# A hybrid encoder layer: memory, x and the S5 parameters laid out by features and by state on the host, packing through three buffers

## The chip, the cores and the metric

The kernel runs on one core of a Trainium2 chip. The metric is device time in microseconds (us) of one execution; a lower figure is better. Times are compared as medians of several runs. The profile is one execution, recorded by the hardware profiler, with the engines TensorE (PE, and PEld for its weight loads), VectorE (DVE), ScalarE (ACT), GpSimd (POOL) and SyncE (SP). SP and POOL also issue DMA transfers, each on a queue of its own.

## The reference

One layer is applied to two groups of tokens, 256 of a prompt and 512 of a sample, together 768 tokens of 1024 features (`TILES = 6` tiles of 128 tokens), each group with a memory of 256 rows of its own (together 512). All is in fp32.

```python
def layer(x, mem, ...):
    h = rmsnorm(x, norm_mix_g)
    u, q, k, v, qm, gl = jnp.split(h @ w_in, SPLITS, axis=-1)
    s5_out   = ...  # bidirectional S5: 64 groups of 16 channels, 64 complex states, + s5_d * u, half-GLU
    diff_out = ...  # differential attention over the tokens, 8 heads
    mem_out  = memory_attention(qm, rmsnorm(mem, mem_norm_g), w_mem_kv, mem_q_g, mem_k_g)
    ...             # branches times w_branch, gates from gl, sum, times w_out, residual, SwiGLU FFN

def memory_attention(q, mem_n, w_kv, q_g, k_g):   # 4 heads of 256
    k, v = jnp.split(mem_n @ w_kv, 2, axis=-1)
    q, k = rmsnorm(q, q_g), rmsnorm(k, k_g)
    p = softmax((q @ k.T) * 256 ** -0.5)
    return p @ v
```

For each of the two directions S5 has `lam`, `dt`, `b` and `c`, with `lam_bar = exp(lam * dt)`, `b_bar = (lam_bar - 1) / lam * b`, and the states `s[t] = lam_bar * s[t-1] + b_bar * u[t]`, `y = real(c * s)`.

## The kernel before, in words

**Products.** Every fp32 operand is split into a high and a low fp32r part, and a product is three matmuls, high x high, high x low, low x high (`mm3`, lines 863 to 865). The splits are made by `split_evac` (853 to 859: high part on ACT, low part on DVE, with a factor per partition where one is given) and, for weights, by `WStream` (547). That class loads weights in halves of 128x1024 on SP's queue through three raw buffers (599), writes the high part on ACT (698) and the low part on DVE (704), in four buffers each, one weight ahead of the one in use (`get`, `ahead`).

**Order.** The program is written for a tile framework that gives every engine a fixed order of instructions, drawn up with a simulated timeline when the program is built; tiles come from pools with a number of buffers each, and an instruction that takes a buffer waits for its last reader. `keep_in_program_order` pins a few instructions to their place. Work of different kinds is interleaved by generators, and a `Pace` (rate times the units done) says when a generator makes a step: `PAR_RATE` for the S5 parameters, `MEM_RATE` for the memory attention, `PACK_RATE` for packing, `S5_RATE` for the S5 steps.

**The stages up to the change's end.**

- *Memory rows* (1087 to 1126). Four row tiles of memory are loaded on SP (`load_rows`, `nx`, six buffers), transposed on PE (1110, `nT`, four 128x128 blocks to a bank), and written with the gain `gmem` as `memThi`/`memTlo`. DVE squares the rows (1124) for the scale `mrs` of each memory row, which is applied later, when K and V leave PSUM.
- *Memory products.* `MEM_ORDER` (796) names twelve units: k0, k1, v0, v1, q0, k2, q1, v2, k3, q2, v3, q3. `mem_k` (957, PSUM `mk`) gives K of a head for four row tiles, `mem_v` (970, `mv`) first scales and normalizes K (with `mrs`) and then gives V (`Vh`, `Vl`), `mem_q` (989, `mq`) gives Q for all 768 tokens from H and transposes K (`kT`). The products of `k0` begin with the first half of the rows, with three filling matmuls (`warm`) ahead of them.
- *x and H* (1132 to 1162). Six row tiles of x are loaded on SP, ACT squares and sums them (885), DVE forms the reciprocal root in twelve small steps (836 to 850) and the normalized rows times gain (`norm_rows`, 906), PE transposes each (`to_features`, 894, `nT`, 48 transposes) beside k1, v0 and v1, and ACT and DVE write `Hhi` and `Hlo` (855, 856).
- *S5 parameters* (`S5.params`, 76). `lam` is loaded on SP, transposed on PE (127, `lamT`), and DVE, ACT and POOL form powers (`pwr`, `pwi`) and factors (`zr`, `zi`, `fr`, `fi`), beside the units k2 to q3 and the memory attention (1021; `ms` scores, `mp`, `mpT` transposes at 1076, `pTh`/`pTl`, `mo` output, stored to DRAM as `mo_scrh`, `mo_scrl`).
- *Raw B and C* (`S5.raws`, 59) are loaded near the end of these units, C on POOL (66), B on SP (73); B's source has 16 contiguous floats (64 bytes) to a piece.
- *Packing* (`S5.pack`, 262), four quarters beside the first two of four chunks of `u` (`u_chunk`, 1189; PSUM `u`). For each: four transposes of C on PE (295, `cT`), their copies on ACT (296), four copies of powers on ACT (301, 302), the diagonal of D and two complex products on DVE (269, pieces through `csc`), all into one buffer `par`, whose store to DRAM (`par_scr`, 312) is issued on SP. A later `fetch` (315) brings back 1/16 of all this at a time (`qd` 0 to 15).
- *S5 steps* (497) beside the rest of `u` and twelve chunks of `gl`: `_outer` (338) forms G (349, `ptG`) and E, then responses (`psK`) and so on.

Behind these follow the differential attention, the branches and the FFN, which the diff doesn't touch.

Of the kernel before, what the change touches and what calls it, by code (L numbers as in the profile page):

```python
# [24 lines left out]
class S5:  # L25
# [15 lines left out]
    def open_dram(self, ctx):  # L41
        tc = self.tc
        self.dr = ctx.enter_context(tc.tile_pool(name="s5d", bufs=1, space=DRAM))
        self.u_scr = [self.dr.tile([128, 8 * NK], F32, name=f"u_scr{m}") for m in range(8)]
        self.k_scr = [self.dr.tile([128, 240], F32, name=f"k_scr{m}") for m in range(16)]
        self.p_scr = [self.dr.tile([128, 4, NPAR], F32, name=f"par_scr{m}") for m in range(4)]
# [4 lines left out]
    @staticmethod  # L51
    def par_views(t):

        f = lambda a, b, **k: t[:, :, a:b].rearrange("p q (g x) -> p q g x", g=4)
        C, B = (t[:, :, o : o + 128].rearrange("p q (g c h) -> p q c g h", g=4, c=2) for o in (0, 128))
        Ar, Ai, Fr, Fi = (f(o, o + 32) for o in range(256, 384, 32))
        return C, B, Ar, Ai, Fr, Fi, t[:, :, 384:400]

    def raws(self, scratch):

        nc, A = self.nc, self.A
        self.craw, self.braw = [], []
        for nm in ("s5_c_re", "s5_c_im"):
            raw = scratch.tile([128, 8, 2, 64], F32, name=nm + "_raw")
            for d in range(2):
                nc.gpsimd.dma_start(raw[:, :, d, :], A[nm][0, d].rearrange("g h p -> (g h) p")
                                    .rearrange("(m q) p -> q m p", q=128))
            self.craw.append(raw)
        for nm in ("s5_b_re", "s5_b_im"):
            raw = scratch.tile([128, 64, 16], F32, name=nm + "_raw")  # L70
            self.braw.append(raw)
            for d in range(2):
                nc.sync.dma_start(raw[64 * d : 64 * d + 64], A[nm][0, d].rearrange("g p h -> p g h"))
                yield

    def params(self, scratch, psA):
# [29 lines left out]
        nc.sync.dma_start(self.kpos, self.consts["kpos"])  # L106
        lraw = []
        for nm in ("s5_lam_re", "s5_lam_im"):
            raw = scratch.tile([64, 2, 64], F32, name=nm + "_raw")
            nc.sync.dma_start(raw, A[nm][0].rearrange("d g p -> g d p"))  # L110
            lraw.append(raw)
        ldt = t("ldt")
        for d in range(2):
            nc.sync.dma_start(ldt[64 * d : 64 * d + 64, :],
                              A["s5_log_dt"][0, d].unsqueeze(0).to_broadcast([64, 64]))
        dcol = scratch.tile([128, 16], F32, name="s5dcol")
        nc.gpsimd.memset(dcol, 0.0)
# [4 lines left out]
        yield  # L122

        lam = []
        for nm, raw in zip(("lre", "lim"), lraw):
            ps = psA("lamT")
            nc.tensor.transpose(ps[:, 0:64], raw.rearrange("g d p -> g (d p)"), env.ident[0:64, 0:64])
            o = t(nm)
            nc.scalar.activation(o, ps[:, 0:64], AF.Copy)
            lam.append(o)  # L130
        lre, lim = lam
# [125 lines left out]
        dv = A["s5_d"][0].rearrange("(q g h) -> g h q", g=4, h=16)  # L257
        for g in range(4):
            nc.sync.dma_start(dcol[32 * g : 32 * g + 16], dv[g])
        self.lam = zr, zi, fr, fi, pwr, pwi, dcol  # L260

    def pack(self, scratch, psA):

        nc, env = self.nc, self.env
# [6 lines left out]
        zr, zi, fr, fi, pwr, pwi, dcol = self.lam  # L271
        split = lambda a: a.rearrange("p (q g) -> p q g", g=4)

        for qt in range(4):
            gs = slice(16 * qt, 16 * qt + 16)
            st = scratch.tile([128, 4, NPAR], F32, name=f"par{qt}", tag="par")
            C, B, Ar, Ai, Fr, Fi, dg = self.par_views(st)
# [13 lines left out]
            ps = psA("cT")  # L291
            for part, (raw, sgn) in enumerate(zip(self.craw, (1.0, -1.0))):
                for m in range(2):
                    o = 256 * part + 128 * m
                    nc.tensor.transpose(ps[:, o : o + 128], raw[:, 2 * qt + m].rearrange("q d p -> q (d p)"), env.ident)
                nc.scalar.activation(C[:, :, part], ps[:, 256 * part : 256 * part + 256]
                                     .rearrange("p (q g h) -> p q g h", g=4, h=16), AF.Copy, scale=sgn)
            yield
# [4 lines left out]
            for g in range(4):  # L303
                r = slice(32 * g, 32 * g + 32)
                tt(dg[r], dcol[r, 4 * qt : 4 * qt + 4].unsqueeze(2).to_broadcast([32, 4, 16]),
                   env.ident[r, 32 * g : 32 * g + 16].unsqueeze(1).to_broadcast([32, 4, 16]), mul)
            yield
            ir, ii = (x[:, gs].rearrange("p (q g) h -> p q g h", g=4) for x in self.braw)
# [421 lines left out]
def hybrid_block(ctx, tc, A, outs, consts):  # L730
# [357 lines left out]
    with tc.tile_pool(name="nrm", bufs=1) as pool, tc.tile_pool(name="nrmg", bufs=1) as pg:  # L1088
# [14 lines left out]
        for t0 in (0, 2):  # L1103
# [12 lines left out]
            if t0 == 0:  # L1116
# [3 lines left out]
                for _ in range(2):  # L1120
                    next(units)
# [1022 lines left out]
```

## Time and profile before

| what | value |
|---|---|
| median of 3 runs (lowest to highest) | 1756.37 us (1753.03 to 1759.49) |
| the profiled execution's own time | 1753.71 us |
| its span in the profile | 1751.9 us |
| mean granted clock of PE | 0.994 |
| DMA packets, bytes, mean rate | 217088, 247.44 MB, 141 GB/s |
| PE busy from 0 to 75 us, of 75.00 | 71.11 us |
| PE busy from 75 to 282.47 us, of 207.47 | 188.16 us |
| PE busy from 282.47 to the end, of 1469.43 | 1459.11 us |

The last three rows are an answer of the trace for three stretches: 75 us is about where Q of the memory attention begins, and at 282.47 us begins the first product behind the last transpose of C. The profile names each group of instructions by line, engine, operation and its tiles as out<-in. A bracket at a row's end holds the time that the engine stood idle before it and what ended this. In rows of the timeline, start and duration come first; matmuls are pipelined, so their durations overlap and their spacing is what counts. A DMA row gives the size of one transfer and the median time from issue to landing. SPq and POOLq are the queues of the issuing engines.

### The profile page before, as it was taken

The numbers are of one execution on the slowest core, as the hardware profiler recorded it, in microseconds if no ns is written. First come the engines' busy times: TensorE is split into PE (matmuls) and PEld (weight loads), VectorE is DVE, ScalarE is ACT, GpSimd is POOL, SyncE is SP. The second block draws the span as 40 slices with busy tenths as digits, with TensorE's granted clock in tenths as the row PEclk, the third lists the DMA queues.
The fourth block names the chain that finished last, engine by engine and source line by source line (L and its number), as shares of the span: only waits on it lengthen the run. The fifth ranks groups of instructions, "written<-read, shape, count | busy, mean of one in ns | idle before, by whom it ended". The sixth has DMA issues, their size and how long they took to land.

```text
span 1751.9 us, 30000 instructions
## 1 busy us (share of the span) xinstructions
PE 1718.4 (98%) x11405; PEld 1588.3 (91%) x11405; DVE 1337.7 (76%) x2486; ACT 941.2 (54%) x1933; POOL 289.1 (16%) x301
## 2 busy tenths in 40 slices
PE   9999897999999999999999999999999999999999
PEld 8989885889888999999998899998889898989897
DVE  6886666899999547898977596894678868787876
ACT  6464442865665436878766464552434544444441
POOL 0000000000000011100111120350023234343430
PEclk9999998999999999999999999999999999999999
DMA  8223655767756636566693445664304547475733
GB/s 256 86 67 109 109 150 156 160 171 186 176 148 174 154 84 150 125 142 146 166 214 106 139 147 165 160 176 146 85 25 120 150 107 180 123 166 133 174 112 108
DMA packets 217088, 247.44 MB, mean 141 GB/s; under 512 B 51304, under 2 KB 171376, under 8 KB 216944
## 3 DMA queue, kind: packets, MB, share of 16 engines
q1 hardware_dynamic: 174208, 155.59, 29.8%
q0 software_dynamic: 31792, 64.76, 19.8%
q10 hardware_dynamic: 10944, 25.17, 4.2%
q8 instruction: 90, 1.47, 0.4%
q14 instruction: 54, 0.44, 0.1%
HBM read 169.84 MB, written 53.35 MB: 127 GB/s over the span
## 4 chain that ended last, share of the span: by engine, by line
PE 81%; issue 11%; DMA 4%; DVE 2%; ACT 2%; POOL 0%; SPq 0%; POOLq 0%; ACTq 0%; DVEq 0%
PE br L864 4%; PE br L865 4%; PE br L863 4%; PE gate L864 3%; PE gate L863 3%; PE gate L865 3%; PE up L863 3%; PE up L864 3%; PE up L865 3%; PE dn L865 3%; PE dn L863 3%; PE dn L864 3%; PE qk L865 3%; PE qk L864 3%; PE qk L863 3%
## 5 line engine op out<-in xcount | busy, mean ns | idle before, releaser
L698 ACT ACTIVATE wh<-wr 128x1024 fp32r<-128x1024 f32 x118 | 133.8, 1138 | 69.5 <-PE gl L864 18.8
L863 PE MATMUL gl<-Hhi,wh 128*128 128x256 f32 (+1 forms) x384 | 132.8, 346 | 0.0
L704 DVE TENSOR_TENSOR wl<-wr,wh 128x1024 fp32r<-128x1024 f32 x72 | 96.1, 1338 | 47.4 <-ACT wh L698 47.0
L865 PE MATMUL gl<-Hhi,wl 128*128 128x256 f32 (+1 forms) x384 | 129.2, 337 | 0.0
L864 PE MATMUL gl<-Hlo,wh 128*128 128x256 f32 (+1 forms) x384 | 128.8, 336 | 0.0
L702 POOL DMA_DIRECT2D wl<-wr x46 | 39.4, 865 | 463.0 <-ACT wl L701 430.9
L863 PE MATMUL qk<-wh,Hhi 128*128 128x256 f32 x384 | 107.6, 280 | 0.0
L864 PE MATMUL qk<-wl,Hhi 128*128 128x256 f32 x384 | 107.6, 280 | 0.0
L865 PE MATMUL qk<-wh,Hlo 128*128 128x256 f32 x384 | 107.2, 279 | 0.0
L618 ACT ACTIVATE wh_S<-ws 128x512 fp32r<-128x512 f32 x91 | 53.9, 625 | 68.1 <-PE up L864 26.6
L623 DVE TENSOR_TENSOR wl_S<-ws,wh_S 128x512 fp32r<-128x512 f32 x91 | 68.0, 768 | 29.0 <-ACT wh_S L618 26.1
L863 PEld LDWEIGHTS gl<-Hhi,wh 128*128 128x128 f32 x384 | 72.1, 188 | 9.5 <-issue 2.2
L865 PEld LDWEIGHTS gl<-Hhi,wl 128*128 128x128 f32 x384 | 72.1, 188 | 8.5 <-issue 0.6
L864 PEld LDWEIGHTS gl<-Hlo,wh 128*128 128x128 f32 x384 | 72.2, 188 | 6.9
L863 PEld LDWEIGHTS qk<-wh,Hhi 128*128 128x128 f32 x384 | 72.3, 188 | 0.8
L865 PEld LDWEIGHTS qk<-wh,Hlo 128*128 128x128 f32 x384 | 72.3, 188 | 0.5
L864 PEld LDWEIGHTS qk<-wl,Hhi 128*128 128x128 f32 x384 | 72.2, 188 | 0.5
L1406 DVE TENSOR_REDUCE nm<-sc 128x1 f32<-128x512 f32 (+1 forms) x96 | 56.6, 597 | 15.1 <-PE sc L1401 14.2
L1408 ACT ACTIVATE p<-sc,nm 128x512 f32<-128x512 f32 (+1 forms) x96 | 59.0, 617 | 12.0 <-DVE nm L1406 11.5
L644 POOL TENSOR_TENSOR ws<-wr,ws 128x512 f32<-128x512 f32 x26 | 39.6, 1524 | 128.2 <-DVE wl_S L623 128.2
L618 ACT ACTIVATE wh_A<-wr 128x512 fp32r<-128x512 f32 x65 | 38.0, 622 | 37.6 <-PE up L864 15.7
L1585 DVE TENSOR_TENSOR fs<-fs,up 128x384 f32<-128x384 f32 x70 | 37.5, 548 | 24.7 <-PE up L865 23.9
(713 smaller groups left out, 6252.3 us busy)
## 6 DMA issues: line engine op xcount, KB each, us to landing
wr<-in_w_in_dram SPq DMA_DIRECT2D x48, 512.0 KB, 4.6
wl<-wr POOLq DMA_DIRECT2D x46, 512.0 KB, 5.5
wr<-in_w_gate_up_dram SPq DMA_DIRECT2D x44, 512.0 KB, 4.0
wr<-in_w_branch_dram SPq DMA_DIRECT2D x24, 512.0 KB, 4.0
wr<-in_w_down_dram SPq DMA_DIRECT2D x22, 512.0 KB, 4.4
wr<-in_w_mem_kv_dram SPq DMA_DIRECT2D x16, 512.0 KB, 3.7
wr<-in_w_in_dram SPq DMA_DIRECT2D x32, 256.0 KB, 4.2
p_scr<-de ACTq DMA_DIRECT2D x27, 256.0 KB, 4.4
```

The source lines that it names most:

```text
L618: self.nc.scalar.activation(f(hi), src, AF.Copy)
L623: self.nc.vector.tensor_tensor(out=f(lo), in0=src, in1=f(hi).bitcast(F32), op=ALU.subtract)
L644: gt(out=s4, in0=A12, in1=s2, op=sub)
L698: self.nc.scalar.activation(hi, r, AF.Copy)
L702: self.nc.gpsimd.dma_start(lo, r.bitcast(F32R), accum_op=ALU.add)
L704: self.sub.tensor_tensor(out=lo, in0=r, in1=hi.bitcast(F32), op=ALU.subtract)
L863: pe.matmul(ps, wh, xh, start=start, stop=False)
L864: pe.matmul(ps, wh, xl, start=False, stop=False)
L865: pe.matmul(ps, wl, xh, start=False, stop=stop)
L1406: v.tensor_reduce(out=nm[:, m : m + 1], in_=ps, axis=AX.X, op=ALU.max, negate=True)
L1408: act.activation(pm[:, 0:n], ps, AF.Exp, bias=nm[:, m : m + 1], accum_out=s1s[:, tt : tt + 1] if m == 0 else s2)
L1585: v.tensor_tensor(out=o, in0=x, in1=y, op=add)
```

## The change

- A new function `layouts` on the host makes `memT` and `xT` (features by tokens), the two gains as columns (`gcols`), `s5_lamT` (real, imaginary, log dt, by state), `s5_bT` (B by state, four quarters), and `s5_cd` (C by state and D's diagonal, 16 pieces).
- Memory features come from `memT` in four tiles on SP. K of head 0 is computed with the features as the outer loop, in four PSUM banks at once, as the features come. The rows of memory are loaded as well, on POOL's queue through two buffers (`load_row`, tag `row`), for the squares alone. The three filling matmuls go.
- x's rows are also loaded on POOL's queue through these two buffers, for the squares alone (ACT). x by features comes in four tiles on POOL's queue in the buffers of `memT`. Each token's reciprocal root is spread over all partitions by PE (ones times a diagonal, 128x128, `rsb`), then DVE multiplies x, gain and `rsb` for each of eight feature blocks of 128x768, and ACT and DVE split that into H.
- `params` loads `s5_lamT` in one transfer on POOL. `pack` loads B by quarters on POOL (two buffers), has no PE work, no C and no diagonal, uses three buffers `par`, stores on POOL, and begins earlier: at the unit where it loaded B and C before (the last units of `MEM_ORDER`), behind the rest of the parameters, at a rate of 0.8 in place of 1.45.
- `fetch` has two transfers on SP: C and diagonal from the input, the rest from what was packed. G's imaginary part is formed with its sign by a `scalar_tensor_tensor` in place of a `tensor_tensor`.

The diff, cut to its core:

```diff
 def params(self, scratch):
-        for nm in ("s5_lam_re", "s5_lam_im"):
-            raw = scratch.tile([64, 2, 64], F32, name=nm + "_raw")
-            nc.sync.dma_start(raw, A[nm][0].rearrange("d g p -> g d p"))
...
-            nc.tensor.transpose(ps[:, 0:64], raw.rearrange("g d p -> g (d p)"), env.ident[0:64, 0:64])
+        lam = scratch.tile([128, 3, 64], F32, name="s5lamT")
+        nc.gpsimd.dma_start(lam, A["s5_lamT"])
...
 def pack(self, scratch):
+        def load(qt):
+            raw = scratch.tile([128, 2, 16, 16], F32, name=f"s5b{qt}", tag="s5b", bufs=2)
+            nc.gpsimd.dma_start(raw, A["s5_bT"][qt])
+            raws.append(raw)
+        load(0)
+        load(1)
+        yield
         for qt in range(4):
-            st = scratch.tile([128, 4, NPAR], F32, name=f"par{qt}", tag="par")
+            st = scratch.tile([128, 4, NPAR - 144], F32, name=f"par{qt}", tag="par", bufs=3)
...
-                    nc.tensor.transpose(ps[:, o : o + 128], raw[:, 2 * qt + m].rearrange("q d p -> q (d p)"), env.ident)
-                nc.scalar.activation(C[:, :, part], ps[:, 256 * part : 256 * part + 256]
-                                     .rearrange("p (q g h) -> p q g h", g=4, h=16), AF.Copy, scale=sgn)
-            yield
             for dst, src in ((Ar, pwr), (Ai, pwi)):
                 lay = lambda x: x[:, :, gs].rearrange("p m (q g) -> p q g m", g=4)
                 nc.scalar.activation(dst[0:64], lay(src[0:64]), AF.Copy)
                 nc.scalar.activation(dst[64:128], lay(src[64:128, ::-1]), AF.Copy)
-            for g in range(4):
-                r = slice(32 * g, 32 * g + 32)
-                tt(dg[r], dcol[r, 4 * qt : 4 * qt + 4].unsqueeze(2).to_broadcast([32, 4, 16]), ...)
-            yield
-            ir, ii = (x[:, gs].rearrange("p (q g) h -> p q g h", g=4) for x in self.braw)
-            cscale(B[:, :, 0], B[:, :, 1], zr, zi, ir, ii, 16)
             yield
             cscale(Fr, Fi, fr, fi, Ar, Ai, 8)
-            nc.sync.dma_start(self.p_scr[qt], st)
+            yield
+            raw = raws[qt].rearrange("p c (q g) h -> p c q g h", g=4)
+            cscale(B[:, :, 0], B[:, :, 1], zr, zi, raw[:, 0], raw[:, 1], 16)
+            nc.gpsimd.dma_start(self.p_scr[qt], st)
+            if qt < 2:
+                load(qt + 2)
             yield
 def fetch(self, qd):
-        self.nc.sync.dma_start(t[:, 0], self.p_scr[hv][:, q])
+        self.nc.sync.dma_start(t[:, 0, 0:144], self.A["s5_cd"][qd])
+        self.nc.sync.dma_start(t[:, 0, 144:], self.p_scr[hv][:, q])
...
-PACK_RATE = 1.45
+PACK_RATE = 0.8
+    def load_row(pool, src, eng):
+        x = pool.tile([128, 1024], F32, name=uid("row"), tag="row", bufs=2)
+        eng.dma_start(x, src)
+        return x
...
+        W._dma()
+        for j in range(4):
+            if j == 2:
+                W._dma()
+            t = pool.tile([128, 2 * TOK], F32, name=f"mt{j}", tag="ft", bufs=4)
...
+            nc.sync.dma_start(t, A["memT"][:, 2 * j : 2 * j + 2])
...
+        pss = [psd("mk"), env.psa("mk"), psd("mk"), env.psa("mk")]
+        for k in range(8):
+            if k % 4 == 0:
+                W.ahead(0, 1 + k // 4)
+            split_evac(MT[0][:, k], MT[1][:, k], mt[k // 2][:, k % 2], cg[:, 0, k : k + 1])
+            w = [x[:, 256 * (k % 4) : 256 * (k % 4) + 256] for x in W.parts[0][k // 4]]
+            for tt in range(4):
+                t = slice(128 * tt, 128 * tt + 128)
+                mm3(pss[tt][:, 0:256], MT[0][:, k, t], MT[1][:, k, t], *w, k == 0, k == 7)
...
         for t in range(4):
-            tc.keep_in_program_order(v.scalar_tensor_tensor(out=xm[t], in0=xm[t], scalar=1.0, in1=xm[t], op0=mul,
+            xm = load_row(pool, ms[t], nc.gpsimd)
+            tc.keep_in_program_order(v.scalar_tensor_tensor(out=xm, in0=xm, scalar=1.0, in1=xm, op0=mul,
                                                             op1=mul, accum_out=mss[:, t : t + 1]))
...
         for tt in range(TILES):
-            to_features(norm_rows(pool, xr[tt], rs[tt], g), H, tt)
-            next(units)
+            xr = load_row(pool, xs[tt], nc.gpsimd)
+            tc.keep_in_program_order(square_sum(xr, pool, ss[:, tt : tt + 1]))
+            if tt % 3 == 2:
+                next(units)
+        for j in range(4):
+            t = pool.tile([128, 2 * TOK], F32, name=f"xt{j}", tag="ft", bufs=4).rearrange("p (k t) -> p k t", k=2)
+            nc.gpsimd.dma_start(t, A["xT"][:, 2 * j : 2 * j + 2])
+            xt.append(t)
+        mean_eps(ss, TILES, 1024)
+        rs = rsqrt(ss, TILES, "xrs")
+        for c0, n in ((0, 512), (512, 256)):
+            ps = env.psa("rsb")
+            for t in range(n // 128):
+                dg = pg.tile([128, 128], F32, name=uid("rsd"), tag="rsd", bufs=2)
+                tt = c0 // 128 + t
+                v.tensor_scalar(out=dg, in0=env.ident, scalar1=rs[:, tt : tt + 1], scalar2=None, op0=mul)
+                pe.matmul(ps[:, 128 * t : 128 * t + 128], ones2, dg, start=True, stop=True)
+            act.activation(rsb[:, c0 : c0 + n], ps[:, 0:n], AF.Copy)
+        for k in range(8):
+            x = xt[k // 2][:, k % 2]
+            v.scalar_tensor_tensor(out=x, in0=x, scalar=cg[:, 1, k : k + 1], in1=rsb, op0=mul, op1=mul)
+            split_evac(H[0][:, k], H[1][:, k], x)
+            next(units, None)
...
             if W.next == 12 and mctx is not None:
                 mctx.close()
                 mctx = None
+                par.drain()
                 scr = uctx.enter_context(tc.tile_pool(name="s5scr", bufs=1))
-                raws = s5.raws(scr)
-            if raws is not None:
-                next(raws, None)
-
-    par.drain()
-    for _ in raws:
-        pass
+                par = Pace(s5.pack(scr), PACK_RATE)
+                next(par.gen)
```

More of the change, by code (lines that the diff above doesn't have):

```diff
@@ L45, in open_dram @@
         self.k_scr = [self.dr.tile([128, 240], F32, name=f"k_scr{m}") for m in range(16)]
-        self.p_scr = [self.dr.tile([128, 4, NPAR], F32, name=f"par_scr{m}") for m in range(4)]
+        self.p_scr = [self.dr.tile([128, 4, NPAR - 144], F32, name=f"par_scr{m}") for m in range(4)]
     def open_work(self, ctx):
@@ L1134, in hybrid_block @@
+        nc.gpsimd.dma_start(gq, A["mem_q_g"][0].unsqueeze(0).to_broadcast([128, 256]))
+        for _ in mem_k(0, pss):
+            pass
         mean_eps(mss, 4, 1024)
@@ L2128 @@
     arrays, A, C = {}, {}, {}
-    for name in _INS:
-        a = np.ascontiguousarray(inputs[name])
+    given = {n: np.asarray(inputs[n]) for n in _INS}
+    laid = layouts(given)
+    for name in [n for n in _INS if n not in _LAID] + list(laid):
+        a = np.ascontiguousarray(laid[name] if name in laid else given[name])
         arrays[f"in_{name}_dram"] = a
```

184 lines of the change are left out of this document (69 added, 115 removed).

## The prediction

> **What bounds the kernel now.** I read the page, then what PE waits for in the first 310 us, then busy time by stretch, then PE, DVE, ACT and the DMA issues in order of time.
>
> ```profile
> span 1751.9 us, 30000 instructions
> PE 1718.4 (98%) x11405; PEld 1588.3 (91%) x11405; DVE 1337.7 (76%) x2486; ACT 941.2 (54%) x1933; POOL 289.1 (16%) x301
> ```
> ```profile
> PE cT L295 <- ACT par L296: 11.7, 1, 11.7
> PE mpT L1076 <- DVE mss L1065: 4.8, 1, 4.8
> ...
> PE u L863 <- ACT par L296: 1.3, 1, 1.3
> ...
> PE mpT L1076 <- DVE mol L856: 0.7, 1, 0.7
> ```
> ```profile
> 200.00:225.00 25.00, 20.80 (x110) 18.20 (x111) 16.56 (x37) 11.54 (x19) 0.28 (x6) 0.93 0.68 110
> ...
> 275.00:300.00 25.00, 18.22 (x96) 15.96 (x97) 12.21 (x26) 4.00 (x8) 0.18 (x3) 0.79 0.51 160
> 300.00:325.00 25.00, 25.00 (x215) 21.75 (x215) 18.13 (x29) 16.23 (x36) 1.97 (x5) 1.00 0.64 139
> ```
>
> PE is full, so time is won by PE work that goes and by PE stalls that go. Nearly half of PE's idle time (1751.9 - 1718.4 = 33.5 us) is in the four waits quoted, 11.7 + 4.8 + 1.3 + 0.7 = 18.5 us, all in the part that the change touches. In the stretches the first pair behind the length is PE's busy time and its instructions, and the last three columns are the granted clock, the DMA engines' share and GB/s: busy time and clock (0.93, 0.79, 1.00) fall with the stalls.
>
> The instructions that the built programs give PE are the same, in the same order, from the first product `u` behind the last `cT` to the end (8,825 instructions). I therefore sum only up to that product, which starts at 282.47 us, and take the rest as unchanged.
>
> ```profile
> 268.34 0.38 PE L295 MATMUL cT<-ident,s_c_im_raw 128*128 128x128 f32 x2
> 280.45 0.69 PE L295 MATMUL cT<-ident,s_c_im_raw 128*128 128x128 f32 x2 [11.73 <-ACT par L296]
> ...
> 283.06 0.41 PE L865 MATMUL u<-Hhi,wl 128*128 128x256 f32 x1
> 283.27 0.41 PE L863 MATMUL u<-Hhi,wh 128*128 128x256 f32 x1
> ...
> 285.86 0.28 PE L864 MATMUL u<-Hlo,wh 128*128 128x256 f32 x1
> 285.97 0.28 PE L865 MATMUL u<-Hhi,wl 128*128 128x256 f32 x1
> ```
>
> A 256-column product follows the last after 0.115 us, and after 0.21 in the three us behind the stall.
>
> **What goes behind H.** ```profile
> 23.02 0.44 PE nT L1110 x4
> ```
> ```profile
> par_scr<-par SPq DMA_DIRECT2D x4, 800.0 KB, 4.6
> ...
> mo_scrh<-moh SPq DMA_DIRECT2D x4, 256.0 KB, 4.7
> ```
>
> The 16 transposes `cT` and the 2 `lamT` leave PE, and with them the wait for one packing buffer whose store (`par_scr`, 4.6 us to landing) had to end first. Four 128-column transposes take 0.44 us, so 1.9 us of work goes. The 4.8 us wait goes too: DVE stood for 5.16 us on `s5_b`, which was loaded in 64-byte pieces and took 12.85 us to land; now each quarter is one contiguous load.
>
> ```profile
> 190.22 12.85 DMA s_b_re_raw<-in_s_b_re_dram
> ...
> 204.20 0.66 PE mpT L1076 x2
> ```
> ```profile
> 203.17 0.43 DVE L269 TENSOR_TENSOR par<-s_b_re_raw,zr 128x256 f32<-128x256 f32 x1 [5.16 <-DMA s_b_re_raw<-in_s_b_re_dram]
> ```
>
> Stalls 18.5, transposes 1.9, and the slow clock behind the two stalls, 14 products at 0.095 each, twice: 2.7. **Goes: 23.1 us.**
>
> **H comes later.** Before, row norms, 48 transposes and the memory products lay side by side on PE, with only 0.2 us of waiting up to `q0`.
>
> ```profile
> 11.00 0.39 PE L863 MATMUL mk<-wh,memThi 128*128 128x256 f32 x1 [1.06 <-ACT memThi L858]
> ```
> ```profile
> 71.03 0.70 DVE Hlo L856
> 71.78 0.66 PE kT L1011 x4
> 72.43 0.24 PE mq L864
> ```
>
> At 72.43 us the 48 narrow products of `q0` were already done (the two prompt blocks, 48 x 0.115 = 5.5), so `q0` from its start would stand at 66.9. Afterwards all products of `q0` need every token's factor `rsb`, and this needs six rows of x that come through two buffers. I follow this chain with these rows:
>
> ```profile
> wr<-in_w_mem_kv_dram SPq DMA_DIRECT2D x11, 512.0 KB, 4.2
> nx<-in_x_sample_dram SPq DMA_DIRECT2D x4, 512.0 KB, 5.1
> ...
> nx<-in_x_prompt_dram SPq DMA_DIRECT2D x2, 512.0 KB, 9.4
> ```
> ```profile
> wl<-wr POOLq DMA_DIRECT2D x46, 512.0 KB, 5.5
> ```
> ```profile
> 32.53 1.22 DVE L704 TENSOR_TENSOR wl<-wr,wh 128x1024 fp32r<-128x1024 f32 x1
> ```
> ```profile
> L885 ACT ACTIVATE njk<-nx 128x1024 f32<-128x1024 f32 x6 | 6.3, 1048 | 0.0
> ```
> ```profile
> 9.53 1.06 ACT L698 ACTIVATE wh<-wr 128x1024 fp32r<-128x1024 f32 x1 [2.14 <-DMA wr<-in_w_mem_kv_dram]
> ```
> ```profile
> 33.86 0.17 DVE L841 TENSOR_SCALAR rqi<-msq 128x4 int32<-128x4 int32 x1
> ```
>
> - The first weights are now the first DMA (0.75 to its issue, an estimate, + 4.2), their high part takes 1.06 and the memory's some 0.6: first product at 7, against 11.0. Four row tiles x 8 x 3 x 0.115 = 11.1 us a head, and some 2 for the second half of weights and features: `k0` ends at 20, `k1` at 31.1.
> - In DVE's order the square of the third memory row stands behind a weight low part whose buffer `k1`'s last products free: 31.1 + 0.4 + 0.6 + 1.05 + 1.2 = 34.3, squared at 35.5. Only then does its buffer take x's first row.
> - Three loads in turn through that buffer, 5.5 to land (POOL's queue) and 1.2 to square on ACT: 42.2, 48.9, 55.6. The other buffer runs behind, between V's high parts in ACT's fixed order: last square at 58.4.
> - In that time V's first products wait for the memory scale (ready at 40.5, read from PSUM behind the first square): PE stands 4 us, and `v1` ends at 59.3, so that this wait is hidden under the chain.
> - Twelve small DVE steps of 0.2, with V and two weight low parts between them, six diagonals in two buffers and the copies: `rsb` at 67.3. DVE's order then has all eight products of x with gain and `rsb` (128x768, from 1.22 per 1024 and an overlap of 0.08: 0.86) ahead of the first `Hlo`: 6.9 + 0.86. **`q0` can run at 75**, and PE has waited about 8.
>
> 75 - 66.9 = **8.1 us later**, and 14 slow products behind the gap: 1.4. All 80 row transposes and the earlier start are inside this term: their 8.8 us is already in the difference of the two starts, so it isn't counted again.
>
> **The packing stretch.** ACT's order now has 12 copies of powers ahead of a `pTh` that had 4 ahead of it.
>
> ```profile
> 193.96 0.43 ACT L302 ACTIVATE par<-pwi 64x128 f32<-64x128 f32 x1
> 194.41 0.60 ACT L855 ACTIVATE pTh<-mpT 128x512 fp32r<-128x512 f32 x1
> ```
> ```profile
> 189.23 0.28 PE L865 MATMUL mv<-wh,memTlo 128*128 128x256 f32 x1
> ```
>
> Eight copies at 0.44 move it to 198.0, its DVE half ends at 199.4, and PE, which has 60 products and 4 transposes (7 us) after 189.3, stands there from 196.3: 3.1 us, and 1 more where DVE's packing holds the next `pTl`. **4.1 new.** If the scheduler's order fits better it is 0; if DVE's packing pieces cost their full 0.43 us (the row with 5.16) and not their spacing of 0.34, 12.
>
> ```profile
> L349 DVE TENSOR_TENSOR ptG<-par x32: 681/684/695, 293.6 to 559.7; 128x512 f32<-128x512 f32 x32
> ...
> L346 DVE TENSOR_TENSOR G<-par x16: 1215/1218/1226, 292.5 to 554.6; 128x1024 f32<-128x1024 f32 x16
> ```
>
> The first response `psK` needs a fetch that waits for the last attention store (4.7 us) and then some 8 us of DVE (two builds of 1.22 + 4 x 0.68): 20 us behind the last `mo`, where PE has 20.3 us of `u`. Cover that thin I price at 1, between 0 and 4. The rest is hidden: 16 more fetches are issued three quarters ahead on SP, and one pass of each `G` takes another form: between no change and twice 0.68, which is 11 us of DVE spread over the 266 us of the row and not on PE's path. I take 0, and keep 2 either way.
>
> **Sum:** 23.1 - 8.1 - 1.4 - 4.1 - 1 = 8.5, say 9 us. The profiled execution took 1753.7 (1.8 outside its span): 1745. The median shown, 1756.4, is 2.7 above it; on that scale **1747 us**.
>
> **The rivals.**
>
> ```profile
> 25.00:50.00 25.00, 25.00 (x222) 25.00 (x221) 22.75 (x90) 18.87 (x43) 0.00 (x0) 1.00 0.60 196
> 50.00:75.00 25.00, 24.77 (x204) 23.94 (x203) 21.67 (x36) 12.17 (x23) 0.28 (x3) 1.00 0.29 88
> ```
>
> - **H on time.** If the rows land in 4.2 (w_mem_kv) and V doesn't stand on the memory scale, three rounds win 4 and the wait another 4; at best `v1` ends at 51 and `q0` starts at 62.5 behind `rsb` and the eight products. Gain 14 to 22: 1734 to 1742. For it: only 0.29 to 0.60 of the DMA engines were busy from 25 to 75 us. Against it: squares, weights and V share two queues in fixed order.
> - **The packing stall stays in another place.** DVE has 24 + 24 packing pieces and four weight parts there: 12 instead of 4, and 4 at `psK`. Gain -2 to 0: 1757. Against it: packing no longer holds PE's own queue.
> - **Slower: rows land late.** Each x row's load starts only when the square two rows back is done, so each us of landing time counts three times. At 5.5 + 9/3 = 8.5 us the gain is gone; that is below the 9.4 of the prompt rows before. At the 12.85 of the slowest load quoted the time is 1747 + 3 x 7.35 = 1769. For it: the same stretch now loads memory (2 MB) and x (3 MB) twice. Against it: the sample rows took 5.1.
>
> The Trainium skill, in "SBUF — State Buffer", section "SBUF: two separate sides", in its box on the DVE trap, says that descriptors of GpSimd's queue wait while DVE holds the shared port, and gives 620 ns becoming about 3100 ns: by that estimate 2.5 us a load, 7.5 in three rounds, 1754. POOL's 46 loads above landed in 5.5 beside a DVE 76% busy, so the trace does not bear it out.
>
> **How the numbers follow.** Sum as forecast (gain 4 to 14, 1742 to 1752) 0.46; H on time 0.23; packing or `psK` 0.18; rows late 0.13, of which 0.09 beyond 0.5%. Half a per cent, 8.8 us, is about what a measurement tells from no change: faster holds 0.23 + 0.26 = 0.49, slower 0.09, within 0.42. The likeliest case's own range is 1742 to 1752; for 8 in 10 the range takes in most of both sides: 1733 to 1760.
>
> **What would show it.** Right: no wait at `cT`; first `mk` near 7; PE idle for about 8 us before a group `mq` between 60 and 76, with DVE busy on 128x768 pieces; a `pTl` wait near 195 of 3 us; the `u` behind the old `cT` place some 9 us earlier. Wrong: x rows landing in 4 or over 8.5 us, a wait at `psK`, or a common tail that differs in length by more than 3 us.

## The result and the profile after

The changed kernel took 1769.1 us (median of 4 runs, 1767.45 to 1771.09) against 1756.7 for the kernel before in the same runs: ratio 1.0072, 95% interval 1.0051 to 1.0094, so 9 to 17 us slower. The forecast was 1747, with 1733 to 1760 as its range, so both the sign and the range were wrong. The profiled execution took 1769.5, its span 1767.7.

The head of the page of the changed kernel, to be laid beside that of before:

```profile
span 1767.7 us, 29778 instructions
PE 1723.5 (97%) x11312; PEld 1589.3 (90%) x11312; DVE 1341.6 (76%) x2453; ACT 934.6 (53%) x1909; POOL 301.0 (17%) x324
```

PE runs 93 instructions fewer and is yet busy 5 us longer, and it stands 44.2 us idle in place of 33.5. What PE waited for in the changed kernel up to 320 us (time in all, times, longest):

```profile
PE mq L831 <- DVE Hlo L823: 5.3, 1, 5.3
PE mk L830 <- ACT wh L665: 4.2, 1, 4.2
PE rsb L1132 <- DVE rsd L1131: 4.2, 3, 2.1
PE mv L830 <- DVE Vl L826: 3.7, 1, 3.7
PE warm L750 <- POOL ident masks.py:199: 3.1, 1, 3.1
PE mq L830 <- ACT Hhi L822: 2.4, 1, 2.4
PE mk L830 <- ACT memThi L825: 2.4, 1, 2.4
PE mo L830 <- ACT pTh L822: 2.2, 1, 2.2
PE psK L343 <- issue: 2.0, 1, 2.0
PE ms L830 <- ACT mp L1039: 1.8, 1, 1.8
```

The waits at `cT` are gone. In their place stand waits on the way to H (`mk`, `mv`, `rsb`, `mq`). By stretch, the changed kernel (columns as before):

```profile
0.00:25.00 25.00, 19.14 (x125) 18.03 (x125) 8.95 (x13) 9.80 (x12) 6.80 (x22) 0.93 0.96 311
25.00:50.00 25.00, 20.33 (x146) 20.13 (x147) 10.43 (x16) 11.53 (x30) 1.59 (x4) 0.86 0.63 200
50.00:75.00 25.00, 18.70 (x156) 18.02 (x154) 17.91 (x75) 14.42 (x26) 2.63 (x5) 1.00 0.60 197
75.00:100.00 25.00, 15.75 (x78) 13.61 (x79) 20.77 (x40) 9.29 (x15) 0.79 (x3) 0.66 0.15 47
...
275.00:300.00 25.00, 25.00 (x140) 21.49 (x139) 8.80 (x12) 8.25 (x11) 0.18 (x3) 1.00 0.55 153
```

From 25 to 50 us PE gave 146 instructions, before 222; from 75 to 100 it gave 78, before 182, at a granted clock of 0.66. From 275 to 300 it is now full, where before it had 18.22 of 25. The starts of the first products of each unit, from PE's timeline, show where time went and came back:

| PE's first product of | before | changed | later by |
|---|---|---|---|
| k1 | 26.9 | 24.5 | -2.4 |
| v0 | 37.9 | 44.1 | 6.2 |
| v1 | 50.6 | 59.3 | 8.7 |
| k2 (q0 is done) | 83.0 | 107.0 | 24.0 |
| q3 | 189.3 | 215.2 | 25.9 |
| third u chunk (behind packing) | 282.5 | 290.7 | 8.2 |
| last half chunk of u | 310.4 | 321.2 | 10.8 |
| end | 1751.9 | 1767.7 | 15.8 |

Three things happened: 24 us lost up to the end of q0, 17.7 won in the packing stretch, and 5 lost behind it, where the products are the same in the same order. The small rest is 1.9 lost between k2 and q3 and 2.6 around the wait at `psK`.

**The way to H.** Three of the loads that GpSimd issued (start, time on the engine, in brackets the wait before), and the transfers issued in the first 24 us (count, size, median time to landing):

```profile
9.80 0.54 POOL L1121 DMA_DIRECT2D xt<-in_xT_dram  x1 [4.46 <-DVE memTlo L826]
...
33.88 0.53 POOL L856 DMA_DIRECT2D row<-in_mem_sample_dram  x1 [11.74 <-DVE row L1094]
...
48.85 0.53 POOL L856 DMA_DIRECT2D row<-in_x_prompt_dram  x1 [13.30 <-DVE row L1094]
```
```profile
xt<-in_xT_dram POOLq DMA_DIRECT2D x4, 768.0 KB, 8.6
wr<-in_w_mem_kv_dram SPq DMA_DIRECT2D x4, 512.0 KB, 9.6
mt<-in_memT_dram SPq DMA_DIRECT2D x4, 512.0 KB, 10.4
row<-in_mem_prompt_dram POOLq DMA_DIRECT2D x2, 512.0 KB, 8.4
```

x by features, needed at 79 us, was fetched from 9.8 on, as soon as the first of memory's features had left its buffer. The scheduler had put these loads ahead of the later rows' in GpSimd's order. With 311 GB/s moving, the weights of the memory products took 9.6 us to land; this is the median of four, and they range from 3.4 to 18.8. The last of the four, the second half of k1's weights, was also issued late. SP's queue stood in the issue of `subg`, a load of 0.5 KB (the kernel before in the first fence, the changed kernel in the second):

```profile
18.85 2.07 SPq L1279 DMA_DIRECT2D subg<-in_diff_sub_g_dram  x1
```
```profile
8.42 14.87 SPq L1251 DMA_DIRECT2D subg<-in_diff_sub_g_dram  x1
23.41 1.75 SPq L566 DMA_DIRECT2D wr<-in_w_mem_kv_dram  x1
```

This half reached ACT at 30.12, and PE's wait of 4.2 us is for it. With x by features late (experiment 4) the issue of `subg` lasts 9.47 us and the half is issued at 17.94. So the early loads cost twice, in landing and in issue. DVE's and ACT's rows show how this went on:

```profile
46.18 1.23 DVE L671 TENSOR_TENSOR wl<-wr,wh 128x1024 fp32r<-128x1024 f32 x1 [1.60 <-ACT wh L665]
47.33 1.22 DVE L1094 SCALAR_TENSOR_TENSOR row<-row 128x1024 f32<-128x1024 f32 x1
...
79.48 7.52 DVE L1136 SCALAR_TENSOR_TENSOR xt<-xt,gcols,rsb 128x768 f32<-128x768 f32 x8 [0.94 <-ACT rsb L1133]
86.92 7.04 DVE L823 TENSOR_TENSOR Hlo<-xt,Hhi 128x768 fp32r<-128x768 f32 x8
```
```profile
54.30 1.06 ACT L852 ACTIVATE njk<-row 128x1024 f32<-128x1024 f32 x1 [7.21 <-DMA row<-in_x_prompt_dram]
...
69.09 1.06 ACT L852 ACTIVATE njk<-row 128x1024 f32<-128x1024 f32 x1 [2.40 <-DMA row<-in_x_sample_dram]
```

The third memory row was squared at 47.33, behind a weight low part at 46.18. Its buffer then fetched x's first row (48.85, squared at 54.30), and x's sixth was squared at 69.09. The factors were ready at 79.48, the first low part of H at 87.8, the last at 94.0.

### The profile page after: what moved, and what is told of

The parts are those of the page before. It is cut to its first block, busy times and chain, and to the rows that moved or that the text cites. A ratio compares the mean times of both kernels' runs of the same rounds, so it can differ in the third digit from the quotient of the medians.

```text
span 1767.7 us, 29778 instructions
## 1 busy us (share of the span) xinstructions
PE 1723.5 (97%) x11312; PEld 1589.3 (90%) x11312; DVE 1341.6 (76%) x2453; ACT 934.6 (53%) x1909; POOL 301.0 (17%) x324
## 4 chain that ended last, share of the span: by engine, by line
PE 76%; issue 15%; DMA 3%; DVE 3%; ACT 2%; POOL 1%; SPq 0%; POOLq 0%; DVEq 0%; ACTq 0%
PE br L831 4%; PE br L830 4%; PE br L832 4%; PE up L830 3%; PE up L831 3%; PE up L832 3%; PE gate L831 3%; PE gate L830 3%; PE gate L832 3%; PE dn L830 3%; PE dn L831 3%; PE dn L832 3%; PE qk L832 3%; PE qk L830 3%; PE qk L831 3%
## 5 line engine op out<-in xcount | busy, mean ns | idle before, releaser
L585 ACT ACTIVATE wh_S<-ws 128x512 fp32r<-128x512 f32 x91 | 54.1, 625 | 63.4 <-PE up L831 27.0
L590 DVE TENSOR_TENSOR wl_A<-wr,wh_A 128x512 fp32r<-128x512 f32 x57 | 51.8, 931 | 6.4 <-ACT wh_A L585 6.4
```

Of the source, the lines that this page charges most:

```text
L585: self.nc.scalar.activation(f(hi), src, AF.Copy)
L590: self.nc.vector.tensor_tensor(out=f(lo), in0=src, in1=f(hi).bitcast(F32), op=ALU.subtract)
```

## The experiments

Each was timed against the kernel before on the same chip; the ratio has its 95% interval. Starts of k1, v0, k2 and so on are those of PE's first product of the unit, in the profile.

**1. The rows of before, the packing of after.** The section between 1090 and 1165 as before; S5 parameters, packing and fetches as changed.

> Rows of memory and x, their transposes and the warm products as before; S5 parameters, packing and fetches as changed. In the changed kernel the stretch from k2 to the fifth half chunk of u (PE's group u 4) took 290.7 - 107.0 = 183.7 us, before 282.5 - 83.0 = 199.5. Theory (the way to H loses about 24 us, packing wins about 16, and the two add up): k2 starts at 83 as before, u 4 near 267, time 1740 to 1744. Rival (packing only looks good because a late H left the other engines ahead): u 4 not before 275, time 1749 to 1757.

1736.9 us, ratio 0.9897 (0.9882 to 0.9912): 18 us faster. k2 starts at 82.6, the third u chunk at 261.4. Its waits from 60 to 300 us:

```profile
PE psK L343 <- issue: 3.1, 1, 3.1
PE mo L830 <- ACT pTh L822: 2.1, 1, 2.1
PE mpT L1051 <- DVE mp L1041: 0.6, 1, 0.6
```

The theory holds, and the gain is larger than it gave: with H on time the new packing wins 18, and the rest of the kernel is as fast as before.

**2. The rows of after, the packing of before.** The reverse.

> Memory and x by features as changed; S5 parameters, packing and fetches as before. Theory (the two parts add up): k2 starts near 107 as in the changed kernel, the waits at cT come back, time 1756.7 + 24 = about 1781 (1777 to 1785). Rival (packing wins only behind a late H, or the late H is made up for later): 1765 to 1772.

1783.4 us, ratio 1.0162 (1.0144 to 1.0179): 28 us slower, k2 at 107.2. The parts add up: -18 and +28 make +10, beside +12 measured for both. Yet 28 is 4 more than k2's 24, and most of these 4 came between 600 and 800 us.

**3. H block by block.**

```diff
-            v.scalar_tensor_tensor(out=x, ...)
-            split_evac(H[0][:, k], H[1][:, k], x)
+            tc.keep_in_program_order(v.scalar_tensor_tensor(out=x, ...))
+            act.activation(H[0][:, k], x, AF.Copy)
+            tc.keep_in_program_order(v.tensor_tensor(out=H[1][:, k], in0=x, in1=H[0][:, k].bitcast(F32), op=sub))
```

> The changed kernel, with the eight products of x, gain and rsb and the eight low parts of H in turn on DVE (in the changed kernel all eight products come first). Theory (the first 24 products of q0 need all eight blocks, and DVE's 16 pieces take 7.5 + 7.0 us in any order): H is complete at 94 as before the edit, the wait of 5.3 us is spread over the blocks, k2 starts within 2 us of 107, time 1767 to 1769. Rival (the order that holds the first low part back costs its wait): k2 5 us earlier, time 1763 to 1765.

1765.8 us, ratio 1.0063 (1.0048 to 1.0078), k2 at 107.8. k2 didn't come earlier, as the theory has it, but for another reason than it gave: H was complete at 99.7, not at 94. The 3 us are in the memory attention behind q1 (v2 at 143.2, before the edit at 147.6) and overlap the changed kernel's interval. What the turn costs DVE is seen in experiment 8.

**4. x by features late.**

```diff
-            nc.gpsimd.dma_start(t, A["xT"][:, 2 * j : 2 * j + 2])
+            tc.keep_in_program_order(nc.gpsimd.dma_start(t, A["xT"][:, 2 * j : 2 * j + 2]))
```

> The changed kernel, with the four loads of x by features (768 KB each) issued behind the last row of x on GpSimd's queue, near 65 us and not between 9.8 and 21.6. Theory (the loads of the first 25 us hold each other up: memory's features took 10.4 us to land, weights of k1 held PE for 4.2): PE waits 4 to 6 us less before V, V's first product starts near 38 to 40 in place of 44.1, the rows' chain moves with it, time 1762 to 1766. Rival (only the rows' chain counts, and it doesn't hang on k0 and k1): k2 stays at 107 or comes later by what x by features then lacks, 1768 to 1775.

1758.4 us, ratio 1.0018 (1.0003 to 1.0034): 10 us off the changed kernel. PE from 25 to 50 us, this kernel:

```profile
25.00:50.00 25.00, 25.00 (x215) 25.00 (x214) 19.82 (x66) 15.88 (x37) 5.42 (x11) 1.00 0.82 257
```

PE is full there, with 215 instructions in place of 146. v0 starts at 35.1 (44.1), v1 at 46.4 (59.3), the first `rsb` at 57.0 (73.4), k2 at 92.9 (107.0). So 14 of the 24 us at k2 came from loads that nobody needed before 79 us. At 803 us this kernel is still 13.9 us ahead of the changed one; of the 3 to 4 us that are missing at the end, the trace shows where they went: near 900 us PE waits 3.6 us for the memory attention's output to be loaded back (2.5 in the changed kernel, see the part on the prediction), with a clock of 0.86 behind it (1.00). The rival falls, and the theory gave too little: the loads held up k0 and k1, and with them the squares behind k1's weight low parts.

**5. Three row buffers.** `bufs=3` in `load_row`, and squares of x in place.

> The changed kernel with three buffers for the second copies of the rows in place of two; to make room, ACT's squares of x write over the row and not into a tile of their own. Theory (the rows' chain through two buffers holds rsb): the third square of memory stands ahead of the weight low parts on DVE, x's rows are squared some 5 to 10 us earlier than at 54.3 to 70.2, rsb near 65 in place of 73.4, time 1759 to 1764. Rival (the loads of the first 25 us and V's place in ACT's order hold rsb anyway): rsb not before 70, 1766 to 1770.

1764.9 us, ratio 1.0052 (1.0033 to 1.0071), the first `rsb` at 71.2, k2 at 103.6. Between the two: the third memory row's load now stands among the first (the second half of k0's weights reached ACT at 17.4 in place of 14.7, and k1 began at 29.9 in place of 24.5), and this takes back some of what the buffer wins; how much was not tried by itself.

**6. 128 unused bytes in the changed kernel.** Of experiment 2's 4 us, 3.6 came between 584 and 803 us, where PE waits for nothing. Products there followed more slowly, at a granted clock of 1.00, and one difference was found in the built programs: the weight buffers start 128 bytes lower, because the pool of small tiles ahead of them shrank.

```diff
-    subg = cp.tile([128, 1], F32, name="subg")
+    subg = cp.tile([128, 1], F32, name="subg"); cp.tile([128, 32], F32, name="gap128")
```

> The changed kernel with 128 unused bytes per partition behind the constants; every engine's instructions and order stay the same. In the changed kernel the weight buffers begin 128 bytes lower than before (wh at 24864, before 24992), because the pool of small tiles shrank, and products with 256 weight columns as the moving side follow each other after 117.8 ns in place of 113.5 (626 to 725 us; the kernel with the rows of before and the packing of after, wh at 24992: 113.4 to 115). Theory (the address of the weight buffers sets this): spacing back to 113.5 to 115 between 25 and 75 and between 640 and 720 us, time 4 to 7 us less, 1762 to 1765. Rival (the spacing comes from something else that the new front does): spacing 117.8 stays, time 1768 to 1770.

1761.2 us (8 runs), ratio 1.0035 (1.0019 to 1.0052). The changed kernel and this one, 20 us of products on weights as the moving side:

```profile
655.00:675.00 20.00, 20.00 (x173) 20.00 (x172) 6.88 (x12) 8.19 (x17) 1.72 (x2) 1.00 0.40 87
```
```profile
655.00:675.00 20.00, 20.00 (x178) 20.00 (x177) 5.38 (x12) 10.69 (x23) 2.28 (x3) 1.00 0.47 107
```

PE is full at clock 1.00 in both, and gives 173 and 178 products. The spacing is 113.5 ns again (114.5 in this stretch). Against the kernel before, this one is 6.7 us late at 320 us, at 600 and at 800, and 5.6 at the end. So the loss behind packing is gone, and with it the assumption that the same instructions take the same time.

**7. 128 and 256 unused bytes in the kernel before.** The same line, 32 and 64 floats.

> The kernel before with the same 128 unused bytes (wh at 25120); instructions and order stay the same. Theory (the address counts, and 128 bytes either way from 24992 are the same): 256-column products on weights follow after 117.8 ns in place of 113.5, time 4 to 8 us more than before. Rival (only the lower address is slow, or the address doesn't count): spacing 113.5, time as before.

> The kernel before with 256 unused bytes ahead of the weight buffers (wh at 25248); instructions and order stay the same. 128 bytes either way gave 117.8 ns between products on 256 weight columns in place of 113.5, and 8 us. Theory (what counts is the start within 256 bytes: 160 is fast, 32 slow; 25248 is 160 again): 113.5 ns between 25 and 50 and between 600 and 650 us, time as before within 2 us. Rival (any other start than 24992 is slow, as by the place relative to H): 117.8 ns, 7 to 9 us more.

128 bytes: 1763.3 us, ratio 1.0048 (1.0032 to 1.0064), 8 us slower with not one instruction changed. 256 bytes: 1755.9 us, ratio 0.9994 (0.9981 to 1.0006). From 640 to 660 us, the kernel before, with 128 and with 256 bytes:

```profile
640.00:660.00 20.00, 20.00 (x179) 20.00 (x178) 9.01 (x17) 7.03 (x13) 1.69 (x2) 1.00 0.44 94
```
```profile
640.00:660.00 20.00, 20.00 (x172) 20.00 (x172) 13.17 (x28) 7.97 (x17) 0.85 (x1) 1.00 0.19 55
```
```profile
640.00:660.00 20.00, 20.00 (x179) 20.00 (x178) 8.86 (x16) 7.03 (x13) 1.69 (x2) 1.00 0.44 95
```

179, 172, 179. Of the four starts tried (24864, 24992, 25120, 25248) the two with a remainder of 160 by 256 are fast, the two with 32 slow. The unused bytes move other buffers as well; that the weights' start is the one that counts is argued from the products that slowed, which all have the weights as the moving side.

**8. All three edits, and with 128 bytes.** Experiments 3, 4 and 5 together, and the gap of 6 on top.

> Three row buffers, x by features loaded behind the rows, and H made block by block, all in the changed kernel. x by features late alone gave 1758.4 (q0 at 67, k2 at 92.9; q0 then waited 5.8 us for the first x by features and 5.3 for the first low part of H). Theory (row chain, early loads and DVE's 15 us of H add up): rsb near 52, k2 at 86 to 89, time 1752 to 1756, still not under the kernel before, because H needs 16 pieces of 0.9 us on DVE behind rsb. Rival (rsb is no longer what q0 waits for): k2 stays at 91 to 93, time 1757 to 1760.

> Three row buffers, x by features late, H by block (1752.6 alone, and 2.5 less than the kernel before), and the 128 bytes that took 8 us off the changed kernel. Theory (the address is a matter of its own and adds): 1743 to 1747. Rival (the faster products only wait longer for H): 1750 to 1753.

1752.6 us, ratio 0.9983 (0.9970 to 0.9996), and 1747.5 us, ratio 0.9938 (0.9916 to 0.9960). The address adds, 5.1 us by the medians and 7.9 by the ratios, where 8 was expected. But rsb came at 57.0 where 52 was expected, and k2 at 95.0 and 93.8, later than with the late loads alone (92.9), where 86 to 89 was expected. So the three edits do not add up as the theory has it, and that 1752.6 lies in its range is luck: what was won over the late loads alone lies behind k2, and why was not tried. Experiment 3's assumption that DVE's pieces take as long in any order fell with it. DVE in the second of them:

```profile
63.17 1.01 DVE L1138 SCALAR_TENSOR_TENSOR xt<-xt,gcols,rsb 128x768 f32<-128x768 f32 x1
65.09 0.96 DVE L1141 TENSOR_TENSOR Hlo<-xt,Hhi 128x768 fp32r<-128x768 f32 x1 [0.91 <-ACT Hhi L1140]
65.97 1.01 DVE L1138 SCALAR_TENSOR_TENSOR xt<-xt,gcols,rsb 128x768 f32<-128x768 f32 x1
```

A block takes 2.80 us in place of 1.8, because DVE stands 0.91 us for ACT's high part. Eight of them are 22.4 us in place of 14.5.

**9. Three low parts on GpSimd.** `low = gp if k in (2, 4, 6) else v` in experiment 8's second kernel.

> The kernel with all three edits and the 128 bytes, with three of H's eight low parts on GpSimd in place of DVE. Theory (behind rsb the time to H is DVE's 16 pieces of some 0.9 us): DVE has 13 pieces left, H is complete 2 to 3 us earlier, k2 too, time 2 to 3 us under the same kernel without this edit (near 1742). Rival (q0 waits for the late x by features, or GpSimd's pieces take over 4 us each and hold H): no change or 1 to 5 us more.

1751.3 us, ratio 0.9963 (0.9948 to 0.9978): 4 us slower than without, though k2 starts 0.8 earlier (92.9). Two places show it. v2 starts at 132.7 in place of 128.8, with another order of PE's products from q0 to k3, and 1.9 us of this are left at the last half chunk of u. Some 3.5 us more are lost near 890 us, where PE waits 3.5 us for the memory attention's output in place of 1.6, with a slower clock behind it (0.94 in place of 1.00 from 875 to 900). What causes either was not tried. A part on GpSimd takes 1.8 us, not the over 4 of the rival:

```profile
71.11 1.82 POOL L1142 TENSOR_TENSOR Hlo<-xt,Hhi 128x768 fp32r<-128x768 f32 x1 [25.07 <-ACT Hhi L1140]
```

**10. Late loads and 128 bytes, with two and with three row buffers, in DVE's first order.**

> X by features late and the 128 bytes, with two row buffers as in the changed kernel; late loads alone gave 1758.4 and k2 at 92.9. Theory (the third row buffer shortens the chain by a few us at most once the loads are late, and the address adds): 1750 to 1753, 6 to 10 more than with three row buffers. Rival (the third buffer does nothing): the same as with three row buffers.

> Three row buffers, x by features late, the 128 bytes, and DVE's order of the changed kernel (all eight products of x, gain and rsb, then the low parts). The same with H made block by block gave 1747.5, with rsb at 55.9, k2 at 93.8, and 22.4 us from the first product to the last low part, because DVE stood 0.91 us in each block for ACT's high part. Theory (that turn between DVE and ACT cost more than it gave once the loads were late): 15 us in place of 22, k2 at 86 to 90, time 1740 to 1744. Rival (the first x by features, late, holds H and not the order): k2 stays at 92 to 95, time 1746 to 1749.

Two buffers: 1751.9 us (11 runs, 1744.6 to 1757.0), ratio 0.9983 (0.9973 to 0.9993), k2 at 92.3. Three: 1746.7 (1743.1 to 1750.4), ratio 0.9947 (0.9928 to 0.9966), k2 at 91.0. The order of 3 did cost DVE its 7 us (H takes 14.5 here), but k2 moves by 2.8 of them, and the time of experiment 8 stays (1747.5). The time is the rival's, and its mechanism is not: x by features had landed by 61.6 us with two buffers and by 58.1 with three, before DVE began H. The same holds for experiment 4 (landed by 61.1, H from 65.0), where the expectation of experiment 8 took q0's wait for one for x by features. DVE begins H at 65.5 with two buffers and at 64.0 with three, right behind the low parts of weights and of K's transposes in its order; ACT's copies of `rsb` end at 64.9 and 63.4, behind or among the high parts of the same. PE waits 6.0 and 4.0 us for the first high part of H. With two buffers the time is 5 us longer by the medians, and the intervals do not meet, near what the theory has. But the profiled execution with two was the fastest of its 11, and the two profiles differ by 0.4 us, so no trace shows where these 5 us lie.

**11. Memory by features, x by rows.** The rows of before with the packing of after, and in the memory part the loop of the change, through the six row buffers:

```diff
+            t = pool.tile([128, 1024], F32, name=uid("nx"), tag="nx", bufs=6)
+            nc.sync.dma_start(t, A["memT"][:, 2 * j : 2 * j + 2])
...
+        for k in range(8):   # split_evac, mm3 into four banks, as in the change
...
+        xm = [load_rows(pool, ms[t]) for t in range(4)]
```

> Memory by features with K of head 0 in four banks as in the changed kernel, memory's rows for the squares, and then x by rows with its transposes as before, all on SP's queue through the six row buffers; packing as changed; weight buffers at 24992. The rows of before with the packing of after gave 1736.9, with k0 from 11.1, k1 from 26.6 and k2 from 82.6. Theory (the loss lies in x by features alone; memory by features starts PE earlier and saves 32 transposes): k1 near 24, k2 at 78 to 81, time 1732 to 1735. Rival (the second copy of memory's rows delays its scale and x's rows): PE waits at V, k2 at 83 to 88, 1737 to 1742.

1734.3 us, ratio 0.9865 (0.9846 to 0.9884), the fastest of all and some 22 us under the kernel before. k1 starts at 19.1 (26.9), v0 at 31.6 (37.9), k2 at 79.8 (83.0). PE's longest waits behind the ones at `warm`, `psK` and `pTh`:

```profile
PE mv L830 <- ACT kr L940: 1.2, 2, 0.6
PE mpT L1051 <- DVE mp L1041: 0.5, 1, 0.5
PE mv L830 <- ACT wh L665: 0.5, 1, 0.5
```

The rival falls: the second copy of memory's rows delays nothing when it comes through six buffers behind the features. The 2.6 us over experiment 1 lie in overlapping intervals; the earlier k1, v0 and k2 are seen.

## Why the prediction was wrong

**What goes behind H: right.** 23.1 us were to go and 4.1 + 1 to come, 18.0 in all; experiment 1 measured 18. The new stalls were 2.1 at `pTh` (3.1 and 1 said) and 3.1 at `psK` (1 said, between 0 and 4). That these two misses cancel is luck; the mechanism of each is in the trace.

**H comes later: the step that failed.** It was put at 8.1 + 1.4 = 9.5 us and was 24.0 (k2). The step named the squares behind a weight low part, the rows' chain and the products ahead of `Hlo`, and all of these are in the trace. But it worked the chain out from "`k0` ends at 20, `k1` at 31.1", with weights that land in 4.2 us, and there it was out by 13: k1 ended at 44.1. The weights took 9.6 us (median), up to 18.8, and the last half of k1's was issued only at 23.41. Of the four loads of x by features the step had only their use, not their issue; they stood ahead of the later rows' loads in the order that the built program gave GpSimd, and 3 MB went through in the time in which the weights of k0 and k1 were due. That these loads made 14 of the 24 us is shown by experiment 4; how the 14 divide between landing and the long issue of `subg` stays open. All behind it is late by about that much: the third square done at 48.5 for 35.5, the last at 70.2 for 58.4, the factors at 79.5 for 67.3, the first low part of H at 87.8 for 75. PE's wait of 4.2 us for weights and the slow clock behind it (0.86 from 25 to 50) belong to it. With the loads late and the weight buffers at their old place (experiment 10, two buffers) k2 is 9.2 us later than before, beside the 9.5 said. So without the early loads the step's chain holds: the last square is done at 53.7 (58.4 said), the factors at 64.9 (67.3), the first low part of H at 73.8 (75). That the sum agrees to 0.3 us is luck, because the rows came 5 us earlier than said and the way from them to k2 took that much longer.

**"I take the rest as unchanged": failed too.** Behind the third u chunk the records of PE name the same products in the same order in both traces (9,560 of them; the prediction counted 8,825 instructions in the built programs), and from the last half chunk of u to the end they took 5 us more. By the starts of the same products the changed kernel is 10.8 us late at 310 us (on the clock of the kernel before), 11.2 at 584, 14.7 at 803, 17.3 at 934 and 16.0 at the last product.

The 3.5 us from 584 to 803 have no wait; their cause is the start of the weight buffers (experiments 6 and 7; with the 128 bytes nothing is lost there). The 2.6 us behind come with a wait for the memory attention's output, which is loaded back from DRAM for the branches (the changed kernel first, then the kernel before):

```profile
PE br L831 <- DMA Hlo<-mo_scrl: 1.8, 1, 1.8
PE br L830 <- DMA Hhi<-mo_scrh: 0.7, 1, 0.7
```
```profile
PE br L864 <- DMA Hlo<-mo_scrl: 0.3, 1, 0.3
```

This wait does not follow the weights' start: it is 0.3 us in the kernel before with 128 bytes (a slow start) and 3.5 in experiment 9 (a fast one). Among the sixteen traces it lies between 0.3 and 3.6 us, and what sets it stays open.

By the two ratios (1.0072 less 1.0035, each known to some 0.2%) the start cost the changed kernel 0.37%, 6.5 us, this wait's difference included, and by experiment 7 the kernel before 8, some of it on the way to H (`mk` and `mv` run on weights as the moving side as well). As a whole: -18 for packing (experiment 1) and +28 for rows, H and address together (experiment 2), of which 6.5 to 8 are the address, make +10, beside +12 with an interval of 9 to 17.

**The rivals.** "Slower: rows land late" had the right sign and the wrong mechanism; that its 1769 is the time measured is luck. x's rows came through GpSimd's queue in 5.4 us (48.85 to 54.30), near the 5.5 that was taken, and the sample rows in 4.2 (median), so the landing that counted three times didn't grow; what came late was the first issue of this chain. What landed late were the weights and memory's features ahead of it, with medians of 9.6 and 10.4 us. The Trainium skill ("SBUF — State Buffer", section "SBUF: two separate sides") has GpSimd unable to write its queue's descriptors while DVE runs an instruction that takes the port they share. The trace doesn't show such a wait: x's rows landed in these 4.2 to 5.5 us while DVE was busy for 17.9 of 25 us (50 to 75). Whether any of DVE's instructions there took that port, no run here shows. "H on time" and "the packing stall stays" did not come.

## What to carry to other kernels

When a load no longer waits for anything, look up where the scheduler puts its issue, and price what else is landing and being issued at that time: 3 MB too early cost 14 us at k2 here. Second copies of an input pay only where the first copy's path was the bound: of this change the packing is worth 18 us and memory by features perhaps a few more, and x by features, with rows through three buffers, gives back some 12 of it even with late loads and the good address (1746.7 beside 1734.3). When equal products take another time, lay their starts side by side to the end of the kernel: stretches without a wait point to the start addresses of the large buffers, and here another 2.5 us lay in a wait 600 us behind the change.

## What the runs showed of the hardware

PE's products on 128x256 weights as the moving side followed each other after 113.5 ns (25 to 75 us in the kernel before; means of 113.3 to 115.3 elsewhere) where the weight buffers began at 160 bytes past a multiple of 256, and after 117.8 ns at 32 bytes past it (117.2 to 117.8 elsewhere; two starts of each kind), PE full and at clock 1.00 both times. Products with H as the moving side and the weights stationary, from 320 to 600 us, didn't change: there the changed kernel stayed 11 us behind the kernel before, and with 128 bytes 6.7, without drift. Over the whole kernel 128 bytes are worth 6.5 to 8 us. Other remainders, and other buffers than the weights', were not tried.

An issue on SP's queue can last as long as a transfer. With 311 GB/s moving in the first 24 us, the issue of a load of 0.5 KB stood on SP for 14.87 us, with the x loads late for 9.47, and in the kernel before for 2.07, and the loads behind it on the queue waited. In the first two it ended (at 23.3 and 17.8 us) within 0.4 us of the time at which ACT received an earlier load of weights of the same queue (23.07 and 18.17). Why it lasts so long is not shown.
